# Layer 1 attention over chosen and near blocks: the loop takes two blocks of weights a step instead of one

## The chip, the cores and the metric

The kernel runs on one core of one Trainium2 chip. The metric is the time of one execution in microseconds. Three executions of the kernel before took 1608.29, 1609.14 and 1612.16 us (median 1609.14).

## The reference, cut to what matters

The program is a two-layer decoder trunk over 1024 tokens of width 1024. Layer 0 is a forgetting attention, layer 1 a sparse attention. In layer 1 each of 16 heads (four heads share keys and values) adds three branches: compressed keys, eight chosen blocks of 64 keys per token, and a window of the last 512 keys.

```python
o_s = softmax(q . k over the chosen blocks) @ v        # chosen
o_w = softmax(q . k over the last 512 keys) @ v        # near
o = g[..., 0:1] * o_c + g[..., 1:2] * o_s + g[..., 2:3] * o_w
x = x + (o.reshape(B, S, W) * silu(z)) @ w_out
```

The change is in the code that computes `o_s` and `o_w`. What is computed is the same before and after.

## The kernel before, in words

The work of layer 1 on `o_s` and `o_w` is cut into 32 "supers", one for each head and each half of 512 queries (`NsaSuper(h, s)`, for each head first s = 1, then s = 0). A super has two parts.

- Eight **units** (L1143), one for each branch and each tile of 128 queries. A unit multiplies queries with keys into a score tile `S_n` (two or four matmuls, L1162, into one of two score buffers of two PSUM banks), VectorE adds the mask and finds the minimum (L1169), ScalarE takes the exponential (L1170), VectorE the reciprocal of the sum (L1172), GpSimd scales by it and the gate (L1174). The weights `P_n` lie with queries on partitions.
- 12 **blocks** for s = 1 and 5 for s = 0, so 17 a head and 272 in all. A block is up to four 128 x 128 pieces of weights. `transposes` (L1180) turns them on TensorE into `ptp_n`, one of two PSUM banks (L1186). `split_t` (L140) then copies the bank to `pth_n` on ScalarE (L143) and writes the rest to `ptl_n` on VectorE (L144); each has four buffers. Only when VectorE has read the bank can the next block but one be transposed into it. `pv` (L1189) multiplies values with both parts into the super's output bank `O_n` (L1194, L1195). `finish` (L1197) reads `O_n` on ScalarE and VectorE (L1204, L1205) and frees it. Output banks are one of two, and the projection of z (`nz`) takes its accumulator from the same two.

`run_attn` (L162) writes these steps in order, with lag = 2 and late = 1: in step x the units of the next super that are due, the transposes of block x, the output products of block x - 2, and the finish of a super whose last block is x - 3. Meanwhile `merge` (L196) weaves in z's projection (`nz_n`, L131 to L133) at a fifth of the cost that the loop yields. The tile framework's scheduler then sets the order on each engine from this program and its own estimates, so instructions may stand in another order than they were written in; each engine runs its own list in order.

Of the kernel before, what the change touches and what calls it, by code (L numbers as in the profile page):

```python
# [38 lines left out]
def tile_fox_nsa(ctx, tc, a, out):  # L39
# [20 lines left out]
    def ps_a(name):  # L60
        return psA.tile([P, 512], F32, tag="A", name=name)
# [100 lines left out]
    def run_attn(supers, lead, lag, late):  # L162


        for u in supers[0].units():
            yield from u
        blocks = [(n, b) for n, x in enumerate(supers) for b in range(len(x.blocks))]
        todo, pend, po, units = 0, {}, {}, []
        for x in range(len(blocks) + lag + late):
            if x < len(blocks):  # L170
                n, b = blocks[x]
                sup = supers[n]
                if b == 0:
                    while todo < len(units):
                        yield from units[todo]
                        todo += 1
                    units, todo = (supers[n + 1].units() if n + 1 < len(supers) else []), 0
                while todo < len(units) and todo * len(sup.blocks) * lead <= b * len(units):
                    yield from units[todo]
                    todo += 1  # L180
                pend[x] = sup.transposes(b)
                yield 450
            if 0 <= x - lag < len(blocks):
                n, b = blocks[x - lag]
                if b == 0:
                    po[n] = ps_a(f"O_{supers[n].name}")
                supers[n].pv(po[n], b, *pend.pop(x - lag))
                yield 450
            if 0 <= x - lag - late < len(blocks):
                n, b = blocks[x - lag - late]  # L190
                if b == len(supers[n].blocks) - 1:
                    yield from supers[n].finish(po.pop(n))

# [67 lines left out]
    pend = []  # L261
# [850 lines left out]
    for qi in range(4):  # L1112
        n = P * (qi + 5)
        bias.append(at.tile([P, n], BF16, name=f"bias{qi}"))
        V.tensor_copy(bias[qi][:, n - P:n], tri)
    class NsaSuper:
# [80 lines left out]
        def finish(self, po):  # L1197
# [15 lines left out]
            yield 0  # L1213

    merge(run_attn([NsaSuper(h, s) for h in range(H) for s in (1, 0)], 0.9, 2, 1), filler, 0.2)
    at.release()
    kv[0].release()
# [110 lines left out]
```

## Time and profile before

| | us |
|---|---|
| median of three executions | 1609.14 |
| the profiled execution | 1609.73 |
| its span (first to last instruction) | 1607.7 |
| stretch of the loop, 1043 to 1505 us | 462 |
| TensorE busy in that stretch | 455.38 |
| VectorE busy in it | 396.13 |
| ScalarE busy in it | 360.80 |
| GpSimd busy in it | 255.88 |

The execution's own time is 2.0 us over the span. All that `run_attn` issues lies in the stretch from 1043 to 1505 us. A busy TensorE is counted from modelled ends of matmuls that overlap, so how fast it goes is read from the distance between the starts of two matmuls in the timeline, and what it waits for from the idle time before a weight load (PEld) or a matmul (PE).

### The profile page before, as it was taken

How to read it: one execution, taken by the hardware profiler on the slowest of the kernel's cores; microseconds unless marked ns; L12 is line 12 of the kernel's file. 1: busy time of each engine (PE TensorE's matmuls, PEld its weight loads, DVE VectorE, ACT ScalarE, POOL GpSimd, SP SyncE). 2: the span in 40 equal slices, each digit the busy share in tenths (PEclk: the TensorE clock that was granted, in tenths of full speed). 3: DMA queues.
4: the chain of work that ended last, by engine and by line, in shares of the span. 5: the costliest groups of instructions: out<-in, count | busy, mean ns of one | idle time of the engine just before them, and what ended most of it. 6: DMA issues, size and time to landing. Idle time of an engine off the chain costs nothing.

```text
span 1607.7 us, 26181 instructions
## 1 busy us (share of the span) xinstructions
PE 1527.3 (95%) x8600; PEld 1269.1 (79%) x8600; DVE 1132.1 (70%) x2867; ACT 870.4 (54%) x2126; POOL 545.1 (34%) x584
## 2 busy tenths in 40 slices
PE   6999999999999868999999989999999999999898
PEld 5887777777777656878888777788888888888786
DVE  6377777777777884355654686788888888888633
ACT  5255545555555662223232545578778778787522
POOL 3232223323223110032333223446646547554200
PEclk9999999999999979999999999999999999999999
DMA  7676666657657675441535645511312312212442
GB/s 241 226 143 134 128 160 131 153 113 149 156 114 160 151 153 165 133 155 60 162 104 154 218 151 193 204 54 63 122 53 66 119 40 79 73 40 93 147 148 92
DMA packets 237431, 209.11 MB, mean 130 GB/s; under 512 B 162737, under 2 KB 184497, under 8 KB 237041
## 3 DMA queue, kind: packets, MB, share of 16 engines
q1 hardware_dynamic: 237296, 207.46, 47.3%
q8 instruction: 68, 1.11, 0.3%
q14 instruction: 67, 0.54, 0.1%
HBM read 123.26 MB, written 46.20 MB: 105 GB/s over the span
## 4 chain that ended last, share of the span: by engine, by line
PE 60%; DVE 18%; ACT 9%; issue 7%; DMA 4%; POOL 1%; SPq 0%; DVEq 0%; POOLq 0%; ACTq 0%
PE ptp_n L1186 6%; PE S_n L1162 6%; DVE P L532 4%; PE y L131 3%; PE y L132 3%; PE y L133 3%; PE O_n L1195 3%; PE O_n L1194 3%; DVE hl L543 3%; ACT P L541 3%; DMA wo<-wD 1%; ACT cP L969 1%; PE nz L131 1%; ACT hl L542 1%; PE nz L132 1%
## 5 line engine op out<-in xcount | busy, mean ns | idle before, releaser
L1174 POOL TENSOR_SCALAR P_n<-P_n,l_n,gates 128x640 f32<-128x640 f32 (+7 forms) x256 | 200.9, 791 | 179.8 <-DVE l_n L1172 146.0
L541 ACT ACTIVATE P<-P,m 128x256 f32<-128x256 f32 (+1 forms) x192 | 117.0, 610 | 164.2 <-DVE m L532 163.8
L144 DVE TENSOR_TENSOR ptl_n<-ptp_n,pth_n 128x512 fp32r<-128x512 f32 (+1 forms) x272 | 181.4, 672 | 33.8 <-ACT pth_n L143 30.1
L1170 ACT ACTIVATE P_n<-P_n,m_n 128x640 f32<-128x640 f32 (+7 forms) x256 | 188.5, 737 | 24.9 <-DVE m_n L1169 22.8
L143 ACT CAST pth_n<-ptp_n 128x512 fp32r<-128x512 f32 (+1 forms) x272 | 153.8, 569 | 72.7 <-PE ptp_n L1186 71.5
L1186 PE MATMUL ptp_n<-ident,P_n 128*128 128x128 f32 x1056 | 167.1, 275 | 5.4 <-DVE ptl_n L144 3.6
L1162 PE MATMUL S_n<-nk,nq 128*128 128x320 f32 (+5 forms) x768 | 171.1, 333 | 0.2 <-DVE m_n L1169 0.2
L512 POOL TENSOR_TENSOR Bd<-B,tri 128x128 f32<-128x128 f32 x128 | 65.0, 509 | 302.3 <-DVE m L532 284.9
L1186 PEld LDWEIGHTS ptp_n<-ident,P_n 128*128 128x128 f32 x1056 | 124.4, 140 | 31.9 <-DVE ptl_n L144 9.3
L1194 PE MATMUL O_n<-pth_n,nv 128*128 128x512 f32 (+3 forms) x384 | 140.1, 369 | 1.0 <-DVE ot_n L1205 0.7
L543 DVE SCALAR_TENSOR_TENSOR hl<-P,hl 128x256 f16<-128x256 f32 (+1 forms) x192 | 126.4, 686 | 19.4 <-ACT hl L542 17.8
L1162 PEld LDWEIGHTS S_n<-nk,nq 128*128 128x128 f32 x768 | 128.0, 188 | 15.2 <-DVE m_n L1169 1.6
L1195 PE MATMUL O_n<-ptl_n,nv 128*128 128x512 f32 (+3 forms) x384 | 120.6, 338 | 0.1
L1169 DVE CUSTOM_DVE_ANT_0 P_n<-S_n,wmask 128x128 f32<-128x128 f32 (+1 forms) x192 | 113.3, 591 | 9.0 <-PE S_n L1162 4.1
L555 PE MATMUL O<-v,pT 128*128 128x192 bf16 x576 | 104.1, 255 | 12.3 <-DMA pT<-hl 10.8
L131 PE MATMUL y<-wo,oh 128*128 128x512 f32 x256 | 103.1, 403 | 9.0 <-ACT oh L627 4.0
L132 PE MATMUL y<-wo,oh 128*128 128x512 f32 x256 | 102.3, 400 | 0.0
L133 PE MATMUL y<-wo,ol 128*128 128x512 f32 x256 | 101.4, 397 | 0.0
L555 PEld LDWEIGHTS <-pT 128*128 128x128 f16 x576 | 57.4, 100 | 54.6 <-issue 40.4
L556 PE MATMUL O<-v,pT 128*128 128x128 bf16 x576 | 97.7, 224 | 0.0
L542 ACT ACTIVATE hl<-P 128x256 f16<-128x256 f32 (+1 forms) x192 | 92.5, 513 | 2.5 <-DMA pT<-hl 0.8
L1194 PEld LDWEIGHTS O_n<-pth_n,nv 128*128 128x128 f32 x384 | 72.6, 189 | 7.0 <-DVE ot_n L1205 1.3
(346 smaller groups left out, 4077.7 us busy)
## 6 DMA issues: line engine op xcount, KB each, us to landing
nq<-qD SPq DMA_DIRECT2D x64, 256.0 KB
B<-cD SPq DMA_DIRECT2D x16, 512.0 KB
wo<-wD SPq DMA_DIRECT2D x16, 512.0 KB
nq<-qD SPq DMA_DIRECT2D x64, 128.0 KB
of<-oF SPq DMA_DIRECT2D x14, 512.0 KB
x<-in_x_dram SPq DMA_DIRECT2D x8, 512.0 KB
wst_k<-in_fox_w_dram SPq DMA_DIRECT2D x8, 512.0 KB
wst_v<-in_fox_w_dram SPq DMA_DIRECT2D x8, 512.0 KB
```

The lines of the kernel that those rows point to most:

```text
L131: T.matmul(ps, wh, mh, start=first, stop=False, **kw)
L132: T.matmul(ps, wh, ml, start=False, stop=False, **kw)
L144: V.tensor_tensor(lo[:, 0:n], pt[:, 0:n], f(hi[:, 0:n]), OP.subtract)
L541: A.activation(L[:, 0:n], L[:, 0:n], AF.Exp, bias=init, scale=-1.0, accum_out=self.lr[:, col + c:col + c + 1])
L543: V.scalar_tensor_tensor(lo[:, cs], L[:, 0:n], UP, hi[:, cs], OP.mult, OP.subtract)
L555: T.matmul(po[:, 0:192], self.hT[:, b0 + k, :], v[:, self.j, k, :], start=(k == 0), stop=False)
L1162: T.matmul(ps[:, b, 0:w], self.q[x][:, qi * P:(qi + 1) * P], k[:, k0 + b * w:k0 + b * w + w], start=(x == 0), stop=(x == 1))
L1170: A.activation(L, L, AF.Exp, bias=m, scale=-1.0, accum_out=lr[:, 0, qi:qi + 1])
L1174: G.tensor_scalar(L, L, lr[:, 1, qi:qi + 1], gates[:, i, x:x + 1], OP.mult, OP.mult)
L1186: T.transpose(pt[:, (x + i) * P:(x + i + 1) * P], L[:, kb * P - k0:(kb + 1) * P - k0], ident)
L1194: T.matmul(po[:, d], v, hi[:, c], start=(b == i == 0), stop=False)
L1195: T.matmul(po[:, d], v, lo[:, c], start=False, stop=(b == len(self.blocks) - 1 and i == len(pieces) - 1))
```

## The change

A step of the loop now takes two blocks: first the units due for both, then the transposes of both (up to eight in a row), then the output products of two blocks, x - 2 and x - 1, then the finishes of blocks x - 3 and x - 2. The yields to `merge` are doubled accordingly. Nothing else is changed; lines behind L187 move down by 2.

```diff
-        for x in range(len(blocks) + lag + late):
-            if x < len(blocks):
-                n, b = blocks[x]
+        for x in range(0, len(blocks) + lag + late, 2):
+            for y in range(x, min(x + 2, len(blocks))):
+                n, b = blocks[y]
...
-                pend[x] = sup.transposes(b)
-                yield 450
-            if 0 <= x - lag < len(blocks):
-                n, b = blocks[x - lag]
+            for y in range(x, min(x + 2, len(blocks))):
+                n, b = blocks[y]
+                pend[y] = supers[n].transposes(b)
+            yield 900
+            for y in range(max(0, x - lag), min(x + 2 - lag, len(blocks))):
+                n, b = blocks[y]
...
-                supers[n].pv(po[n], b, *pend.pop(x - lag))
-                yield 450
-            if 0 <= x - lag - late < len(blocks):
-                n, b = blocks[x - lag - late]
+                supers[n].pv(po[n], b, *pend.pop(y))
+            yield 900
+            for y in range(max(0, x - lag - late), min(x + 2 - lag - late, len(blocks))):
+                n, b = blocks[y]
```

In the two programs' lists of instructions the first difference on any engine lies in this loop, and behind it the lists are the same again from the first part of the output projection on. In the names below, `n4_1` is head 4, half s = 1, and a further number is the block or, for `P` and `S`, the branch and the query tile.

The first place is TensorE in the middle of head 1, s = 1. Before, from the transposes of block 5:

```order
L1186 MATMUL ptp_n1_1_5_11106<-ident_72,P_n1_1_1_0_10913 128x128
L1186 MATMUL ptp_n1_1_5_11106<-ident_72,P_n1_1_1_1_10927 128x128
L1186 MATMUL ptp_n1_1_5_11106<-ident_72,P_n1_1_1_2_10949 128x128
L1186 MATMUL ptp_n1_1_5_11106<-ident_72,P_n1_1_1_3_10960 128x128
L131 MATMUL nz1_1_10989<-hT1_1_0_6788,whi_nz1_10397 128x512
L132 MATMUL nz1_1_10989<-hT1_1_1_6789,whi_nz1_10397 128x512
L133 MATMUL nz1_1_10989<-hT1_1_0_6788,wlo_nz1_10398 128x512
L1194 MATMUL O_n1_1_11060<-pth_n1_1_3_11080,nv_0_0_10388 128x512
L1195 MATMUL O_n1_1_11060<-ptl_n1_1_3_11081,nv_0_0_10388 128x512
L1162 MATMUL S_n1_0_1_0_11120<-nk_0_1_10390,nq0_1_0_10997 128x128
L1162 MATMUL S_n1_0_1_0_11120<-nk_0_1_10390,nq1_1_0_10998 128x128
L1186 MATMUL ptp_n1_1_6_11129<-ident_72,P_n1_1_1_0_10913 128x128
```

And in the changed kernel, from the transposes of the same block:

```order
L1188 MATMUL ptp_n1_1_5_11118<-ident_72,P_n1_1_1_0_10898 128x128
L1188 MATMUL ptp_n1_1_5_11118<-ident_72,P_n1_1_1_1_10912 128x128
L1188 MATMUL ptp_n1_1_5_11118<-ident_72,P_n1_1_1_2_10949 128x128
L1188 MATMUL ptp_n1_1_5_11118<-ident_72,P_n1_1_1_3_10974 128x128
L1188 MATMUL ptp_n1_1_6_11127<-ident_72,P_n1_1_1_0_10898 128x128
L1188 MATMUL ptp_n1_1_6_11127<-ident_72,P_n1_1_1_1_10912 128x128
L1188 MATMUL ptp_n1_1_6_11127<-ident_72,P_n1_1_1_2_10949 128x128
L1188 MATMUL ptp_n1_1_6_11127<-ident_72,P_n1_1_1_3_10974 128x128
L1196 MATMUL O_n1_1_11060<-pth_n1_1_3_11080,nv_0_0_10388 128x512
L1197 MATMUL O_n1_1_11060<-ptl_n1_1_3_11081,nv_0_0_10388 128x512
L1196 MATMUL O_n1_1_11060<-pth_n1_1_4_11089,nv_0_0_10388 128x512
L1197 MATMUL O_n1_1_11060<-ptl_n1_1_4_11090,nv_0_0_10388 128x512
```

The transposes of blocks 5 and 6 now stand together, and the output products of blocks 3 and 4 behind them.

The second place is VectorE at the border between the two halves of head 4, right behind the split of block 1 of s = 0. Before:

```order
L1205 SCALAR_TENSOR_TENSOR ot_n4_1_12575<-O_n4_1_12304,ot_n4_1_12575 64x512
L1169 ISA P_n5_1_0_2_12542,m_n5_1_0_2_12543<-S_n5_1_0_2_12541,bias2_10483 128x896
L1169 ISA m_n5_1_0_2_12543 128x1
L1172 RECIPROCAL l_n5_1_0_12490<-l_n5_1_0_12490 128x1
L1169 ISA P_n5_1_0_3_12553,m_n5_1_0_3_12554<-S_n5_1_0_3_12552,bias3_10485 128x1024
L1169 ISA m_n5_1_0_3_12554 128x1
L1172 RECIPROCAL l_n5_1_0_12490<-l_n5_1_0_12490 128x1
L1169 ISA P_n5_1_1_0_12579,m_n5_1_1_0_12580<-S_n5_1_1_0_12578,wmask_10475 128x640
L1169 ISA m_n5_1_1_0_12580 128x1
L144 TENSOR_TENSOR ptl_n4_0_2_12569<-ptp_n4_0_2_12563,pth_n4_0_2_12568 128x512
```

And in the changed kernel, at the same place:

```order
L1171 ISA P_n5_1_0_2_12542,m_n5_1_0_2_12543<-S_n5_1_0_2_12541,bias2_10483 128x896
L1171 ISA m_n5_1_0_2_12543 128x1
L1171 ISA P_n5_1_0_3_12553,m_n5_1_0_3_12554<-S_n5_1_0_3_12552,bias3_10485 128x1024
L1171 ISA m_n5_1_0_3_12554 128x1
L1171 ISA P_n5_1_1_0_12564,m_n5_1_1_0_12565<-S_n5_1_1_0_12563,wmask_10475 128x640
L1171 ISA m_n5_1_1_0_12565 128x1
L1174 RECIPROCAL l_n5_1_0_12490<-l_n5_1_0_12490 128x1
L1171 ISA P_n5_1_1_1_12575,m_n5_1_1_1_12576<-S_n5_1_1_1_12574,wmask_10475 128x640
L1171 ISA m_n5_1_1_1_12576 128x1
L1174 RECIPROCAL l_n5_1_0_12490<-l_n5_1_0_12490 128x1
L144 TENSOR_TENSOR ptl_n4_0_2_12594<-ptp_n4_0_2_12588,pth_n4_0_2_12593 128x512
L1207 SCALAR_TENSOR_TENSOR ot_n4_1_12611<-O_n4_1_12325,ot_n4_1_12611 64x512
```

The finish of the earlier half (`ot_n4_1`) has moved from right behind the split of block 1 to behind the split of block 2, past four score tiles and two reciprocals.

The third place is TensorE at the loop's end, from the last block's transposes on. Before:

```order
L1186 MATMUL ptp_n15_0_4_17120<-ident_72,P_n15_0_0_2_16912 128x128
L1186 MATMUL ptp_n15_0_4_17120<-ident_72,P_n15_0_0_3_16943 128x128
L1186 MATMUL ptp_n15_0_4_17120<-ident_72,P_n15_0_1_2_17014 128x128
L1186 MATMUL ptp_n15_0_4_17120<-ident_72,P_n15_0_1_3_17036 128x128
L1194 MATMUL O_n15_0_17101<-pth_n15_0_2_17097,nv_3_0_15145 128x384
L1195 MATMUL O_n15_0_17101<-ptl_n15_0_2_17098,nv_3_0_15145 128x384
L1194 MATMUL O_n15_0_17101<-pth_n15_0_2_17097,nv_3_0_15145 128x128
L1195 MATMUL O_n15_0_17101<-ptl_n15_0_2_17098,nv_3_0_15145 128x128
L1194 MATMUL O_n15_0_17101<-pth_n15_0_3_17114,nv_3_1_15149 128x384
L1195 MATMUL O_n15_0_17101<-ptl_n15_0_3_17115,nv_3_1_15149 128x384
L1194 MATMUL O_n15_0_17101<-pth_n15_0_3_17114,nv_3_1_15149 128x128
L1195 MATMUL O_n15_0_17101<-ptl_n15_0_3_17115,nv_3_1_15149 128x128
```

And in the changed kernel, at the same place:

```order
L1188 MATMUL ptp_n15_0_4_17118<-ident_72,P_n15_0_0_2_16912 128x128
L1188 MATMUL ptp_n15_0_4_17118<-ident_72,P_n15_0_0_3_16943 128x128
L1188 MATMUL ptp_n15_0_4_17118<-ident_72,P_n15_0_1_2_17014 128x128
L1188 MATMUL ptp_n15_0_4_17118<-ident_72,P_n15_0_1_3_17023 128x128
L1196 MATMUL O_n15_0_17101<-pth_n15_0_1_17086,nv_3_1_15136 128x512
L1197 MATMUL O_n15_0_17101<-ptl_n15_0_1_17087,nv_3_1_15136 128x512
L1196 MATMUL O_n15_0_17101<-pth_n15_0_2_17095,nv_3_0_15132 128x384
L1197 MATMUL O_n15_0_17101<-ptl_n15_0_2_17096,nv_3_0_15132 128x384
L1196 MATMUL O_n15_0_17101<-pth_n15_0_2_17095,nv_3_0_15132 128x128
L1197 MATMUL O_n15_0_17101<-ptl_n15_0_2_17096,nv_3_0_15132 128x128
L1196 MATMUL O_n15_0_17101<-pth_n15_0_3_17114,nv_3_1_15136 128x384
L1197 MATMUL O_n15_0_17101<-ptl_n15_0_3_17115,nv_3_1_15136 128x384
```

The output products of block 1 have moved behind the last transposes.

## Rows read from the trace of the kernel before

**Rows 1.** The page's busy time, share of the span and instructions of each engine.

```profile
PE 1527.3 (95%) x8600; PEld 1269.1 (79%) x8600; DVE 1132.1 (70%) x2867; ACT 870.4 (54%) x2126; POOL 545.1 (34%) x584
```

**Rows 2.** Windows: stretch and length, busy of PE, PEld, DVE, ACT, POOL, clock, DMA.

```profile
1043.00:1505.00 462.00, 455.38 (x2877) 400.40 (x2877) 396.13 (x1074) 360.80 (x820) 255.88 (x298) 1.00 0.22 72
...
1522.00:1530.00 8.00, 8.00 (x24) 6.24 (x24) 2.89 (x6) 3.46 (x7) 0.00 (x0) 0.64 0.59 163
```

**Rows 3.** Timeline, TensorE: start, length, engine, line, operation, tiles, shape, count.

```profile
1210.87 0.60 PE L1186 MATMUL ptp_n<-ident,P_n 128*128 128x128 f32 x4
1211.22 0.42 PE L1194 MATMUL O_n<-pth_n,nv 128*128 128x384 f32 x1
1211.48 0.33 PE L1195 MATMUL O_n<-ptl_n,nv 128*128 128x384 f32 x1
1211.65 0.22 PE L1194 MATMUL O_n<-pth_n,nv 128*128 128x128 f32 x1
1211.71 0.27 PE L1195 MATMUL O_n<-ptl_n,nv 128*128 128x128 f32 x1
1211.82 0.39 PE L1162 MATMUL S_n<-nk,nq 128*128 128x128 f32 x2
...
1212.33 0.39 PE L132 MATMUL nz<-hT,whi_nz 128*128 128x512 f32 x1
1212.56 0.40 PE L133 MATMUL nz<-hT,wlo_nz 128*128 128x512 f32 x1
```

**Rows 4.** Timeline, TensorE, near the loop's end.

```profile
1494.91 0.28 PE L1195 MATMUL O_n<-ptl_n,nv 128*128 128x128 f32 x1
1495.02 0.41 PE L1186 MATMUL ptp_n<-ident,P_n 128*128 128x128 f32 x2
```

**Rows 5.** Waits of weight loads in the loop's stretch: us in total, times, longest.

```profile
PEld ptp_n L1186 <- DVE ptl_n L144: 9.3, 28, 1.0
...
PEld S_n L1162 <- DVE m_n L1169: 1.6, 7, 0.5
PEld O_n L1194 <- DVE ot_n L1205: 1.3, 3, 0.8
```

**Rows 6.** Timeline, 1154.7 to 1157.3 us: a split that comes late.

```profile
1154.71 0.64 PE L1186 MATMUL ptp_n<-ident,P_n 128*128 128x128 f32 x4
...
1155.28 1.05 ACT L143 CAST pth_n<-ptp_n 128x512 fp32r<-128x512 f32 x2
...
1155.87 1.29 DVE L144 TENSOR_TENSOR ptl_n<-ptp_n,pth_n 128x512 fp32r<-128x512 f32 x2 [0.31 <-ACT pth_n L143]
...
1156.62 0.66 PE L1186 MATMUL ptp_n<-ident,P_n 128*128 128x128 f32 x4 [0.57 <-DVE ptl_n L144]
```

**Rows 7.** Timeline, the loop's last output products.

```profile
1502.22 0.69 DVE L144 TENSOR_TENSOR ptl_n<-ptp_n,pth_n 128x512 fp32r<-128x512 f32 x1 [1.00 <-ACT pth_n L143]
...
1502.50 0.33 PE L1194 MATMUL O_n<-pth_n,nv 128*128 128x256 f32 x1
...
1502.97 0.39 PE L1195 MATMUL O_n<-ptl_n,nv 128*128 128x256 f32 x1
```

**Rows 8.** Groups by line in the loop's stretch: busy us, mean ns, idle before.

```profile
L144 DVE TENSOR_TENSOR ptl_n<-ptp_n,pth_n 128x512 fp32r<-128x512 f32 (+1 forms) x272 | 181.4, 672 | 33.8 <-ACT pth_n L143 30.1
...
L1186 PE MATMUL ptp_n<-ident,P_n 128*128 128x128 f32 x1048 | 165.4, 275 | 5.2 <-DVE ptl_n L144 3.6 <-DVE l_n L1172 0.7 <-POOL P_n L1174 0.5
...
L1169 DVE CUSTOM_DVE_ANT_0 P_n<-S_n,bias 128x640 f32<-128x640 f32 (+3 forms) x60 | 61.0, 1017 | 4.1 <-PE ptp_n L1186 3.3 <-POOL P_n L1174 0.4
...
L1172 DVE RECIPROCAL l_n<-l_n 128x1 f32<-128x1 f32 x249 | 39.2, 158 | 15.0 <-ACT P_n L1170 11.8
L1205 DVE SCALAR_TENSOR_TENSOR ot_n<-O_n,ot_n 64x512 f32<-64x512 f32 x32 | 21.7, 678 | 1.8 <-ACT ot_n L1204 1.3
```

**Rows 9.** Timeline, VectorE: a score tile of 640 columns.

```profile
1210.59 0.82 DVE L1169 CUSTOM_DVE_ANT_0 P_n<-S_n,wmask 128x640 f32<-128x640 f32 x1 [0.37 <-POOL P_n L1174]
```

**Rows 10.** Timeline, TensorE: its first matmul behind 3.5 us of idle time.

```profile
1521.57 0.76 PE L131 MATMUL y<-wo,oh 128*128 128x512 f32 x1 [3.54 <-DVE xr L638]
```

## The prediction

> **What bounds the kernel now.** I read the page's busy shares first: TensorE leads with 95% of the span [rows 1]. Then the windows, since a mean over the span says little of one loop: in the loop's 462 us TensorE is busy for 455.38 us, VectorE for 396.13 (86%), ScalarE for 360.80, GpSimd for 255.88, at a granted clock of 1.00 [rows 2]. The reader is to see that TensorE never rests for long there and that VectorE is the next one, with 66 us of room. Then the timeline of TensorE, start to start. A matmul of 512 columns takes 0.23 us, one of 384 0.17, one of 128 0.06 when its partner follows [rows 3]; that is about 0.45 ns a column. Four transposes with the first output product of 384 columns take 0.61 us (1210.87 to 1211.48), which is 4 x 0.11 + 0.17: leaving a run of transposes costs nothing. Entering one costs 0.05 us where the matmul ahead has 128 columns (0.11 instead of 0.06 [rows 4]; the same before a score matmul [rows 3]), and nothing where it has more, since the next weight load then hides behind it.
>
> Last the waits. What weight loads wait for in the loop is small: 9.3 us in 28 places for the split on VectorE that empties the transposes' bank, 1.6 us for a score bank, 1.3 us for an output bank [rows 5]. How a late split looks: the casts of two blocks run back to back in 1.05 us behind exponentials, their VectorE halves take 1.29 us, and TensorE stands for 0.57 us before the transposes that need the first of the two banks [rows 6]. So the loop is bound by TensorE's own work, and the change does not touch the amount of that: the same 272 blocks, 256 units and matmuls. It can win or lose on borders between kinds of work and on waits.
>
> **The change part by part.**
> Borders. Counted in the two lists of TensorE's instructions, the loop enters a run of transposes 297 times before and 211 times now. Right behind a matmul of 128 columns it did so 56 times and does so 18 times: 38 x 0.05 = 1.9 us less. Matmuls of 128 columns ahead of a score or a z matmul go from 50 to 42: 8 x 0.05 = 0.4 us less. Together **-2.3 us**. The other borders cost nothing by the rows above, and bound the term: nothing is saved if weight loads turn out to be late all the same, and 4.3 us if each of the 86 entries that go is worth 0.05.
>
> The scheduler does the change by about half: 74 runs of six to eight transposes come out, 110 of four stay. That is in the counts above.
>
> Waits for the split. With the spacings above I added up TensorE's work between the end of a block's transposes and the start of those of the next block but one, which need its bank. Under 1.8 us there are 35 places before and 35 now; under 1.6 us there are 7 and 12. Five more tight places at the mean wait of 9.3 / 28 = 0.33 us are **+1.7 us**. In pairs the second block is not the tight one: under 1.8 us it stands once. Bounds: the 9.3 us go altogether, or each of the 74 pairs waits once for 0.57 us as at 1156.62, 42 us. I take the value near the first end, since the distances hardly move.
>
> Waits for score banks. Two units in a row stand 55 times in the new list, 18 times in the old; VectorE needs 0.67 us for a split and about 1.1 us for a large score tile [rows 8], so units in a row lean on the two score buffers. The distance from a unit to the next but one is under 1.0 us in 6 places instead of 5: 1.6 us x 6/5, **+0.3 us**. Bounds: -1.6 us, and 37 more double units at 1.6 / 7 = 0.23 us, +8.5 us.
>
> Waits of output products for the split. Between a block's transposes and its products TensorE now has 3.6 us of work in the middle of the distribution instead of 2.9. That hides what little is waited for; at the very end the last block's second product starts 0.47 us behind the first where 0.12 are due, because its split ends at 1502.91 [rows 7]. Two more products stand between now: **-0.3 us**.
>
> Other queues. No DMA is added; those that units and finishes issue on SP's queue move with them by a block at most, and in the loop the DMA engines are busy for 22% [rows 2]. Loads that the output projection waits for are set off by z's last matmul, which is the last TensorE work of the loop in both lists, so the end moves with TensorE. GpSimd has the scaling of weights in the same order; its room is 206 us.
>
> Sum: -2.3 + 1.7 + 0.3 - 0.3 = -0.6 us. Against the profiled execution's 1609.73 us that is 1609.1; it ran 0.6 us above the median of the three, so I predict **1608.5 us**.
>
> **The rivals.**
> *The waits go.* If a longer path between transposes and products lets the splits run ahead, the 9.3 us for the bank, the 1.3 us for output banks and most of the 1.6 us go: 12 us less, and no 2.0 us of new ones. 1608.5 - 14 is 1595 at most; with half of it 1601. For it: products wait less by the counts. Against: the bank's distances are no longer than before, and the bank, not the products, is where most is waited for.
>
> *The finish comes late at the middle of a head (slower).* In heads 2, 4, ... 14 the border between the halves falls between two pairs. There the list of VectorE has the finish behind two splits, four score tiles, two reciprocals and a third split. The queue from block 0's split on is 3 x 0.67 + 2 x (1.02 + 0.08) + 2 x (0.82 + 0.08) + 3 x 0.16 + 0.68 = 7.2 us [rows 8, 9] (0.08 us is what reading the minimum adds), and at its head two more score tiles of 1.1 us each are still under way, some 1.3 us of them. So the output bank is free some 8.5 us after the transposes of block 0 start. TensorE has until then 19 transposes, six products, six units and ten z matmuls, 9.2 us by the spacings, and then wants the bank. The margin is 0.7 us. It decides from there: VectorE also waits in this stretch, for casts (33.8 us of idle time before splits in the loop) and exponentials (15.0 before reciprocals) [rows 8]. If it slips by 2 us, TensorE stands 1.3 us at seven heads and about as much for the score banks behind it, 9 us: 1617.5 us.
>
> *The change does nothing* because the scheduler pulls the pairs apart again: 1609 us. Against it, 74 long runs.
>
> *The clock falls.* Granted were 1.00 in the whole loop, where runs of four transposes (0.44 us) stand between matmuls; behind 3.54 us of idle TensorE at 1521.57 [rows 10] the clock went to the lower level (1.2 GHz), 0.64 on average over 8 us [rows 2], a loss of 2.9 us. Runs of eight would need 0.88 us without another matmul, far from that idle time; if the clock fell once a head, 16 x 2.9 = 46 us, 1655 us. The Trainium skill ("TensorE: Matmul & The Clock Gate", Part 4: PE-mode transpose) says that a transpose does not count as TensorE activity for the clock gate and takes about 275 ns in a kernel. The mean here is 275 ns [rows 8], as it says; that transposes let the clock fall no run here shows, and by that rule this rival would come true where runs double.
>
> **How the numbers follow.** A change below 0.3% (4.8 us) cannot be told from none. Forecast 0.66 and the change that does nothing 0.08, both within 0.3% (1604.3 to 1614.0), less 0.01 for the forecast's own edge below it: same 0.73. The waits go 0.12, with that edge faster 0.13. The late finish 0.12 and the clock 0.02: slower 0.14. The forecast's own range is 1604 to 1613. For 8 in 10 I reach a third into each of the two likelier rivals: 1601 to 1616, which leaves out about 0.18.
>
> **What would show it.** In the changed profile: the loop's stretch again 459 to 466 us at a clock of 1.00; transposes in runs of eight at 0.11 us start to start; the wait of weight loads for the split (L144) between 8 and 14 us, for score banks about 2; the last products 0.12 us apart. If the waits for the split fall below 5 us the first rival is right; if products wait for the finish (L1207) for over 5 us, or score matmuls for the minimum (L1171), the second. I am wrong if the stretch differs by over 5 us, or if the difference lies outside of it.

## The result and the profile after

The changed kernel takes 1617.51 us (median of six runs, 1615.64 to 1619.63), the kernel before 1608.72 in the same comparison: 1.0053 times as long, with a 95% interval of 1.0038 to 1.0068. It is 8.8 us slower, outside of the range that was forecast and on the other side. Its profiled execution took 1619.63 us.

First the page's busy line of the changed kernel, to be laid beside [rows 1]:

```profile
PE 1537.7 (95%) x8600; PEld 1270.4 (79%) x8600; DVE 1135.4 (70%) x2867; ACT 865.8 (54%) x2126; POOL 547.6 (34%) x584
```

Then the windows between two landmarks that both kernels have, from the first output product behind the first 384- and 512-column score tiles of head 0 to the first matmul of the output projection (columns as in [rows 2]). Before:

```profile
1043.04:1505.95 462.91, 456.30 (x2880) 401.16 (x2881) 396.09 (x1074) 360.76 (x820) 256.77 (x299) 1.00 0.22 72
```

After:

```profile
1044.86:1519.29 474.43, 464.38 (x2881) 401.94 (x2881) 399.24 (x1074) 356.52 (x821) 256.84 (x298) 1.00 0.22 70
```

The same instructions take 11.5 us longer, at the same clock. So the loss lies in the loop. (Each kernel left one profile, so these are two single executions.) Outside of it the two profiles differ by +1.8 us ahead and -3.1 us behind; in the profiles taken below the first transposes stand anywhere from 1033 to 1040 us in kernels that differ only behind them, and the stretch behind the loop takes 97 to 102 us, so one pair of profiles says nothing there.

What TensorE waits for in that stretch after (us in total, times, longest; before: [rows 5]):

```profile
PEld ptp_n L1188 <- DVE ptl_n L144: 11.2, 34, 0.7
PEld S_n L1164 <- DVE m_n L1171: 6.7, 23, 1.1
PE ptp_n L1188 <- DVE ptl_n L144: 6.4, 21, 0.5
PEld ptp_n L1188 <- POOL P_n L1176: 5.6, 13, 0.7
PEld O_n L1196 <- DVE ot_n L1207: 2.0, 8, 0.3
```

These rows are not yet the loss: a weight load's wait (PEld) counts even where a matmul still runs in front of it, and what the matmul behind it waits stands in a row of its own (PE). The row with POOL P_n names GpSimd, but wherever a block's first transpose comes over 0.05 us late in the loop, its weights were scaled before the bank's split ended; it is the bank there, too. I took the distance between the starts of neighbouring matmuls over the loop and subtracted the spacings of [rows 3, 4]. What is left over, before and after, in us, by the matmul that starts late:

| late matmul | before | after |
|---|---|---|
| first transpose of a block right behind another block's transposes | 0.2 (3 places) | 5.3 (20) |
| other transposes inside a run (0.05 each, mostly) | 1.5 | 2.5 |
| first transpose behind another kind of work | 10.7 | 11.2 |
| product behind a product | 1.6 | 5.3 |
| score matmul | 4.8 | 7.5 |
| all (with z and the rest) | 24.3 | 38.0 |

That is 13.7 us more, and the spacings themselves sum to some 2 us less. Of the transposes' 12.4 and 19.0 us, the split that empties the bank accounts for 11.5 and 18.4. Two places show the two rows that grew most. The first, on ScalarE, VectorE and TensorE, from 1441.83 us:

```profile
1441.83 0.58 ACT L143 CAST pth_n<-ptp_n 128x512 fp32r<-128x512 f32 x1
...
1442.30 0.73 ACT L1172 ACTIVATE P_n<-P_n,m_n 128x512 f32<-128x512 f32 x1
...
1443.01 0.58 ACT L143 CAST pth_n<-ptp_n 128x512 fp32r<-128x512 f32 x1
...
1443.61 0.38 PE L1188 MATMUL ptp_n<-ident,P_n 128*128 128x128 f32 x2
1443.62 0.69 DVE L144 TENSOR_TENSOR ptl_n<-ptp_n,pth_n 128x512 fp32r<-128x512 f32 x1 [0.28 <-ACT pth_n L143]
...
1444.46 0.63 PE L1188 MATMUL ptp_n<-ident,P_n 128*128 128x128 f32 x4 [0.47 <-DVE ptl_n L144]
```

The pair's first block has two transposes, which start at 1443.61, so the second block's four are due at 1443.83. But the bank that they need still holds the second block of the pair before. Its cast stands on ScalarE behind the first one's cast and behind an exponential; it starts at 1443.01, VectorE's half behind it ends at 1444.31, and TensorE goes on at 1444.46, 0.63 us late.

Other work in the queue is the rule. In 16 places a pair's second block starts over 0.1 us late, 5.1 us in sum. In 14 of them (4.7 us) something else stands ahead of the split that empties the bank, which ends 2.0 to 3.3 us behind its last transpose: on ScalarE exponentials in ten places and the read of an output bank in one, on VectorE score tiles in three. Only two places (0.4 us) show the bare chain of cast and VectorE half, 1.57 us.

The second place, TensorE's products of two blocks:

```profile
1323.45 0.22 PE L1196 MATMUL O_n<-pth_n,nv 128*128 128x128 f32 x1
1323.51 0.27 PE L1197 MATMUL O_n<-ptl_n,nv 128*128 128x128 f32 x1
1323.62 0.39 PE L1196 MATMUL O_n<-pth_n,nv 128*128 128x384 f32 x1
1323.85 0.34 PE L1197 MATMUL O_n<-ptl_n,nv 128*128 128x384 f32 x1
```

The 128-column product at 1323.51 is followed after 0.11 us instead of 0.06, and the next block's 384-column product takes 0.23 instead of 0.17. A product right behind another block's 128-column product stands 42 times in the loop now and stood 6 times before: 0.05 us each, and 0.055 more in the 26 where 384 columns follow, 0.05 more in the 16 where 256 do (0.17 instead of 0.12 us).

### The profile page after: what moved, and what is told of

Its sections match the earlier page's. It is cut to its first block, busy times and chain, and to the rows that moved or that the text cites. A ratio compares the mean times of both kernels' runs of the same rounds, so it can differ in the third digit from the quotient of the medians.

```text
span 1617.9 us, 26138 instructions
## 1 busy us (share of the span) xinstructions
PE 1537.7 (95%) x8600; PEld 1270.4 (79%) x8600; DVE 1135.4 (70%) x2867; ACT 865.8 (54%) x2126; POOL 547.6 (34%) x584
## 4 chain that ended last, share of the span: by engine, by line
PE 60%; DVE 19%; ACT 9%; issue 6%; DMA 4%; POOL 1%; SPq 0%; DVEq 0%; ACTq 0%; POOLq 0%
PE S_n L1164 7%; PE ptp_n L1188 6%; DVE P L534 4%; PE y L131 3%; PE y L132 3%; PE y L133 3%; PE O_n L1196 3%; PE O_n L1197 3%; DVE hl L545 3%; ACT P L543 3%; ACT cP L971 1%; ACT hl L544 1%; PE nz L131 1%; PE nz L132 1%; PE nz L133 1%
## 5 line engine op out<-in xcount | busy, mean ns | idle before, releaser
L144 DVE TENSOR_TENSOR ptl_n<-ptp_n,pth_n 128x512 fp32r<-128x512 f32 (+1 forms) x272 | 180.0, 671 | 37.8 <-ACT pth_n L143 35.8
L1164 PE MATMUL S_n<-nk,nq 128*128 128x320 f32 (+5 forms) x768 | 165.5, 334 | 1.2 <-DVE m_n L1171 1.0
L1188 PE MATMUL ptp_n<-ident,P_n 128*128 128x128 f32 x1056 | 156.0, 276 | 7.8 <-DVE ptl_n L144 6.4
L1188 PEld LDWEIGHTS ptp_n<-ident,P_n 128*128 128x128 f32 x1056 | 121.0, 141 | 35.1 <-DVE ptl_n L144 11.2
L1196 PE MATMUL O_n<-pth_n,nv 128*128 128x512 f32 (+3 forms) x384 | 131.7, 352 | 0.1
L557 PE MATMUL O<-v,pT 128*128 128x192 bf16 x576 | 104.0, 255 | 12.7 <-DMA pT<-hl 11.2
```

The costliest lines, as they stand in the source:

```text
L144: V.tensor_tensor(lo[:, 0:n], pt[:, 0:n], f(hi[:, 0:n]), OP.subtract)
L1164: T.matmul(ps[:, b, 0:w], self.q[x][:, qi * P:(qi + 1) * P], k[:, k0 + b * w:k0 + b * w + w], start=(x == 0), stop=(x == 1))
L1188: T.transpose(pt[:, (x + i) * P:(x + i + 1) * P], L[:, kb * P - k0:(kb + 1) * P - k0], ident)
L1196: T.matmul(po[:, d], v, hi[:, c], start=(b == i == 0), stop=False)
```

## The experiments

Theory 1: the second block of a pair waits for its bank, because splits queue up. Theory 2: borders between products cost time. The rivals stand in the expectations. Fifteen kernels ran; times are medians, and ratios are to the kernel before on the same chip (1607.7 to 1609.1 us).

**Which part of the step costs time.** Four kernels. *Units alone in twos*:

```diff
-            for y in range(x, min(x + 2, len(blocks))):
-                n, b = blocks[y]
-                pend[y] = supers[n].transposes(b)
-            yield 900
...
+            for d in range(2):
+                y = x + d
+                if y < len(blocks):
+                    n, b = blocks[y]
+                    pend[y] = supers[n].transposes(b)
+                    yield 450
+                y -= lag
+                if 0 <= y < len(blocks):
...
+                    supers[n].pv(po[n], b, *pend.pop(y))
+                    yield 450
```

> Only the units come in twos: a step issues the units of two blocks, then block x's transposes, the output products of block x - 2, block x + 1's transposes and the products of x - 1. In TensorE's list 17 pairs of blocks have their transposes side by side (before 5, changed kernel 81), 5 products stand right behind another block's 128-column product (6 and 42), and two units in a row stand 51 times (18 and 55). Theory 1 (the second block of a pair waits for its bank, because VectorE needs 0.67 us a split and TensorE only 0.44 us for four transposes: 7.7 us of such waits in the changed kernel, 1.4 before) and theory 2 (products of two blocks side by side expose a weight load, 0.05 us in 42 places and 0.055 more in 28, some 3.3 us): within 3 us of the kernel before, 1607 to 1612. Rival 3 (score banks, because units come in twos): as slow as the changed kernel, 1615 to 1619.

Measured: 1609.79 us, 1.0005 (0.9994 to 1.0017). No loss that can be told, so units in twos alone do not make the changed kernel slow, as rival 3 had it. They are not free, though. In this kernel's profile the loop, from its first transpose to the projection, is 3.5 us longer than before; weight loads wait 8.2 us for score banks instead of 1.6 [rows 5], and first transposes behind another kind of work start 8.2 us late in sum instead of 10.7:

```profile
PEld S_n L1167 <- DVE m_n L1174: 8.2, 23, 1.1
```

*Output products alone in twos*:

```diff
             for y in range(x, min(x + 2, len(blocks))):
...
                     todo += 1
-            for y in range(x, min(x + 2, len(blocks))):
-                n, b = blocks[y]
                 pend[y] = supers[n].transposes(b)
-            yield 900
+                yield 450
```

> Only the output products come in twos: units and transposes of each block stand together as before, two blocks a step, and then come the products of two blocks. 28 pairs of transposes side by side, 40 products behind another block's 128-column product, two units in a row 20 times. By the spacings of the kernel before TensorE's work without waits is 2.8 us shorter. Theory 1: the waits of second blocks fall from 7.7 to about 3 us; with theory 2's 3.3 us the time is that of the kernel before within 2.5 us, 1607 to 1611. If theory 2 held alone, as slow as the changed kernel (1615 to 1619); if theory 1 held alone, 1604 to 1608. Rival 3: no loss.

Measured: 1614.68 us, 1.0037 (1.0026 to 1.0047). More than forecast, and neither theory's number. Products behind products lose 4.6 us, nearly what they lose in the changed kernel, and second blocks only 1.1. But first blocks lose 15.3 us instead of 10.7, which no theory had said.

*Transposes in twos, products apart*, with the second block's products behind the next step's units; units come in twos here too:

```diff
...
+            for y in range(max(0, x - lag - 1), min(x - lag, len(blocks))):
+                n, b = blocks[y]
...
+                supers[n].pv(po[n], b, *pend.pop(y))
+                yield 450
             for y in range(x, min(x + 2, len(blocks))):
                 n, b = blocks[y]
                 pend[y] = supers[n].transposes(b)
             yield 900
-            for y in range(max(0, x - lag), min(x + 2 - lag, len(blocks))):
+            for y in range(max(0, x - lag), min(x + 1 - lag, len(blocks))):
...
```

> Only the transposes come in twos: the products of the second block of a step are issued behind the next step's units, so products are apart. 87 pairs of transposes side by side, 14 products behind another block's 128-column product, two units in a row 49 times; the distance from a block's transposes to those of the next block but one is under 1.6 us in 28 places (changed kernel 12). Theory 1: slow, 1614 to 1620, with waits of second blocks of 7 us or more. Theory 2 alone: 1607 to 1611.

Measured: 1623.36 us, 1.0093 (1.0076 to 1.0111), slower than the changed kernel. Second blocks lose 5.6 us, as theory 1 says; the score banks lose much too, so this is not the price of transposes in twos alone. Its row of waits for them, beside 1.6 us before [rows 5]:

```profile
PEld S_n L1170 <- DVE m_n L1177: 13.5, 39, 1.1
```

*Pairs that start anew at each head*:

```diff
-        for x in range(0, len(blocks) + lag + late, 2):
-            for y in range(x, min(x + 2, len(blocks))):
+        starts = [v for v in range(len(blocks)) if v % 17 % 2 == 0]
+        groups = [list(range(v, w)) for v, w in zip(starts, starts[1:] + [len(blocks)])]
...
+        for i in range(len(groups) + 2):
+            for y in groups[i] if i < len(groups) else ():
...
```

> The changed kernel, but the pairs start anew at each head: 17 blocks are eight pairs and a single one, so that no pair of an odd head straddles the border between two halves or two heads. 80 pairs of transposes side by side, 34 products behind another block's 128-column product, two units in a row 62 times. Theories 1 and 2: as slow as the changed kernel, 1615 to 1620 (distances under 1.6 us: 27 instead of 12). Rival 4 (the loss comes where pairs straddle, in the odd heads: in the trace a pair of heads loses 1.6 us, all of it between the starts of an odd head and the next): 1608 to 1611.

Measured: 1616.65 us, 1.0050 (1.0034 to 1.0067). The loss stays, so it does not hang on pairs that straddle a border.

**More pairs.** *Products ahead of the transposes in a step*:

```diff
-            for y in range(x, min(x + 2, len(blocks))):
-                n, b = blocks[y]
-                pend[y] = supers[n].transposes(b)
-            yield 900
             for y in range(max(0, x - lag), min(x + 2 - lag, len(blocks))):
...
                 supers[n].pv(po[n], b, *pend.pop(y))
             yield 900
+            for y in range(x, min(x + 2, len(blocks))):
+                n, b = blocks[y]
+                pend[y] = supers[n].transposes(b)
+            yield 900
```

> The changed kernel with a step's products ahead of its transposes. The list has more pairs: 109 blocks' transposes stand right behind another's (changed kernel 81), 40 products behind another block's 128-column product. Theory 1: waits of second blocks grow with their number, from 7.7 to about 10 us: 1617 to 1623. If pairing as such were not the cause but the place of the products, no slower than the changed kernel: under 1616.

Measured: 1633.89 us, 1.0160 (1.0144 to 1.0176). Slower than any theory had it, and by another wait: second blocks lose 1.0 us, but products now come before their weights are split. What changed is the distance, not the split: from a block's last transpose to its first product there are 1.99 us in the median instead of the changed kernel's 4.03, and the split ends 1.97 us behind that transpose instead of 2.00.

```profile
PEld O_n L1196 <- ACT pth_n L143: 20.3, 57, 0.8
PEld O_n L1197 <- DVE ptl_n L144: 9.1, 33, 0.5
```

So this kernel says nothing for or against theory 1; it shows that products need the distance that the changed kernel's order gives them.

**Is it the split?** Each of the next four alterations was made to both kernels, and the gap between the two is what tells. *VectorE's half reads the rounded copy instead of the bank*:

```diff
-            return split_t(at, pt, n * P, f"{self.name}_{b}")
...
+            A.copy(hi[:, 0:n * P], pt[:, 0:n * P])
+            V.tensor_tensor(lo[:, 0:n * P], f(hi[:, 0:n * P]), f(hi[:, 0:n * P]), OP.subtract)
...
```

> The kernel before, in which VectorE's half of the split reads the rounded copy twice instead of the transposes' bank, so that the second part of the weights is zero and the bank is free behind ScalarE's cast. All instructions stay in number. The cast ends some 0.85 us behind the last transpose instead of 1.74 for the split, so the 11.5 us that transposes wait for banks go nearly all: 1597 to 1601.

> The same alteration of the changed kernel. Theory 1 and 2: the 18.4 us of bank waits go, the 3.3 us of exposed loads between products stay, so the kernel is 2 to 4 us slower than the altered kernel before: 1599 to 1605. Rival 5 (it is not the banks: what pairing costs lies in the longer stretches without transposes or units, on GpSimd and the score banks): the gap to the altered kernel before stays 8 us or more.

Measured: 1639.18 (1.0192, 1.0176 to 1.0208) and 1646.83 us (1.0236, 1.0220 to 1.0252). Both were slower by far, so the pair is no clean test. The gap between the two stayed at 7.7 us by the medians, just under the 8 of rival 5, though no bank waited for VectorE's half. The groups by line of the altered kernel before (busy us, mean ns) show what got slower:

```profile
L1174 POOL TENSOR_SCALAR P_n<-P_n,l_n,gates 128x512 f32<-128x512 f32 (+2 forms) x235 | 242.7, 1039 | 136.7 <-DVE l_n L1172 101.0 <-PE ptp_n L1186 13.8 <-PE S_n L1162 9.1
L1190 DVE TENSOR_TENSOR ptl_n<-pth_n 128x512 fp32r<-128x512 f32 (+1 forms) x252 | 210.3, 840 | 24.2 <-ACT pth_n L1189 21.8
```

The same group on GpSimd in the kernel before, where VectorE reads one of its two inputs from the bank (its own half: [rows 8], 672 ns):

```profile
L1174 POOL TENSOR_SCALAR P_n<-P_n,l_n,gates 128x384 f32<-128x384 f32 (+2 forms) x250 | 195.1, 787 | 175.1 <-DVE l_n L1172 141.3 <-PE ptp_n L1186 18.4 <-PE S_n L1162 15.0
```

With both inputs in SBUF, VectorE's half takes 840 ns and GpSimd's scaling 1039 instead of 787.

*No reciprocals on VectorE*:

```diff
-            V.reciprocal(lr[:, 1, qi:qi + 1], lr[:, 0, qi:qi + 1])
             x = 3 * h + 1 + y
-            G.tensor_scalar(L, L, lr[:, 1, qi:qi + 1], gates[:, i, x:x + 1], OP.mult, OP.mult)
+            G.tensor_scalar(L, L, lr[:, 0, qi:qi + 1], gates[:, i, x:x + 1], OP.mult, OP.mult)
```

> The kernel before without VectorE's 256 reciprocals (GpSimd scales by the sum itself, so the weights are scaled wrongly): 40 us less work in VectorE's queue, and no waiting for an exponential there. TensorE's work is the same. Bank waits fall from 11.5 us to 6 to 9, score-bank waits to under 2: 1603 to 1608.

> The same alteration of the changed kernel, with 80 pairs of transposes side by side and 39 products behind another block's 128-column product. Theory 1a (the second block waits for the chain itself: two casts of 0.57 us and two VectorE halves of 0.67 us back to back behind transposes that follow each other in 0.44 us, however free VectorE is): waits of second blocks stay at 6 us or more, the gap to the altered kernel before at 6 to 10 us: 1610 to 1617. Theory 1b (VectorE's queue of other work makes the second split late): these waits fall below 4 us and the gap to the 2 to 5 us of the borders: 1606 to 1612.

Measured: 1609.03 (0.9999, 0.9986 to 1.0011) and 1618.42 us (1.0056, 1.0038 to 1.0075). A gap of 9.4 us, so these 40 us of VectorE's other work are not the cause of it. Theory 1b holds in half at most: second blocks did fall below 4 us, to 3.5, but the gap did not fall. The kernel before did not get faster, against my forecast for it.

*VectorE's half over half of the columns*, with second parts in four tiles zeroed ahead of the loop:

```diff
-            return split_t(at, pt, n * P, f"{self.name}_{b}")
...
+            A.copy(hi[:, 0:n * P], pt[:, 0:n * P])
+            V.tensor_tensor(lo[:, 0:n * 64], pt[:, 0:n * 64], f(hi[:, 0:n * 64]), OP.subtract)
...
```

> The kernel before, in which VectorE's half of the split covers only the first half of a block's columns (the other columns of the second part stay zero): some 0.37 us instead of 0.67, 272 times, still read from the transposes' bank. TensorE's and ScalarE's work stay. A lone block's bank is free 0.3 us sooner: bank waits fall from 11.5 us to 2 to 5, 1600 to 1606.

> The same alteration of the changed kernel. The list has 114 pairs of transposes side by side (changed kernel 81). Theory 1a (a second block waits for the chain of two casts and two VectorE halves): the second half now ends 0.37 us behind the second cast, some 1.35 us behind the block's last transpose instead of 1.8, so waits of second blocks fall from 7.7 to under 3 us, in spite of more pairs, and the gap to the altered kernel before to the borders' 2 to 5 us: 1602 to 1610. If the second blocks' waits have another cause: a gap of 8 us or more.

Measured: 1607.95 (0.9995, 0.9983 to 1.0006) and 1617.50 us (1.0053, 1.0038 to 1.0067). The half took 0.41 us, not 0.37, as the group by line of the altered changed kernel shows:

```profile
L1197 DVE TENSOR_TENSOR ptl_n<-ptp_n,pth_n 128x256 fp32r<-128x256 f32 (+1 forms) x265 | 108.6, 413 | 53.3 <-ACT pth_n L1196 50.3
```

In the profiles the loop, from its first transpose to the projection, is 3.6 and 5.8 us shorter than without the alteration, but the zeroing on VectorE stands ahead of it, and the whole times did not move. The gap stayed at 9.5 us. Here theory 1a failed: the gap should have fallen to 2 to 5 us, and second blocks, 114 of them instead of 81, still lose 3.8 us.

*No VectorE half at all*:

```diff
-            return split_t(at, pt, n * P, f"{self.name}_{b}")
...
+            A.copy(hi[:, 0:n * P], pt[:, 0:n * P])
+            return hi, zlo
```

> The kernel before without VectorE's half of the split: the second part of the weights is one tile of zeros, and the products with it still run. TensorE's and ScalarE's work stay, VectorE has 181 us less, and a bank is free behind ScalarE's cast, some 0.85 us behind the last transpose. Nothing is read twice from SBUF, so GpSimd is not slowed as in the kernel that read the rounded copy twice. The waits for banks go (11.5 us) and most of the score banks': 1595 to 1600.

> The same alteration of the changed kernel; 125 pairs of transposes side by side. By the spacings its list is 3.9 us shorter than that of the altered kernel before, and the borders between products cost some 3.5 us. If what pairing costs beyond the borders lies in the queue of splits, on ScalarE and VectorE: within 3 us of the altered kernel before, 1595 to 1602. If it lies elsewhere: a gap of 7 us or more.

Measured: 1605.76 (0.9980, 0.9969 to 0.9991) and 1607.83 us (1.0001, 0.9990 to 1.0011). The gap falls from 0.53% to 0.21%, or from 8.8 to 2.1 us by the medians, although this list has 125 pairs instead of 81 and the same borders. What waits for the split is now ScalarE's cast alone, in the changed kernel:

```profile
PEld ptp_n L1191 <- ACT pth_n L1193: 5.1, 8, 0.8
PE ptp_n L1191 <- ACT pth_n L1193: 4.2, 9, 0.6
```

But it is not the second blocks' waits that went. They are 4.2 us here (5.3 in the changed kernel), nearly all in seven places, and in each of the seven exponentials stand on ScalarE ahead of the cast that is waited for. The loop's gap went from 11.6 to 4.1 us in the profiles, and over half of that at products behind another kind of work, because the kernel before loses more there without VectorE's half: they start 7.3 us late in sum instead of 2.7, much of it for output banks, and in the changed kernel 2.5 instead of 1.8. The altered kernel before:

```profile
PEld O_n L1199 <- DVE ot_n L1210: 5.8, 13, 0.6
```

So the smaller gap does not show that the loss goes through VectorE's half. That the kernel before got only some 3 us faster, where 9 to 14 were forecast, fits with this: its 11.5 us of bank waits were in good part replaced by others.

**Attempts at a faster kernel**, both one block a step. *Units a little later*, lead 1.0 instead of 0.9:

```diff
-    merge(run_attn([NsaSuper(h, s) for h in range(H) for s in (1, 0)], 0.9, 2, 1), filler, 0.2)
+    merge(run_attn([NsaSuper(h, s) for h in range(H) for s in (1, 0)], 1.0, 2, 1), filler, 0.2)
```

> An attempt at a faster kernel: one block a step as before, with units due a little later (lead 1.0 instead of 0.9). The distance from a block's transposes to those of the next block but one is under 1.8 us in 25 places instead of 35; 34 products stand behind another block's wide product, where nothing is exposed. Theory 1: some 3 us less of bank waits, 1604 to 1608. If the distances don't decide: 1607 to 1611.

Measured: 1612.70 us, 1.0029 (1.0017 to 1.0041), slower: the transposes' bank waits were 12.5 us instead of 11.5 in spite of the longer distances.

*More of z's work behind the transposes that wait*:

```diff
                 pend[x] = sup.transposes(b)
-                yield 450
+                yield 1800 if len(sup.blocks) == 12 and b in (1, 2, 7) else 181
```

> An attempt at a faster kernel, one block a step as before: the loop yields more behind the transposes of blocks 1, 2 and 7 of each s = 1 half and less behind the others, so that z's matmuls stand where transposes wait for banks. The distance from a block's transposes to those of the next block but one is under 1.8 us in 21 places instead of 35, under 1.6 in 4 instead of 7, all else in the list as before. Theory 1: bank waits fall from 11.5 us to some 8, 1604 to 1608. If the waits only move: 1608 to 1611.

Measured: 1607.27 us, 0.9993 (0.9979 to 1.0007), no difference that can be told. The bank waits fell to 7.8 us, and the products' waits for the output bank rose (weight loads for L1205: 1.3 [rows 5] to 3.7 us). Neither of the two beat the kernel before.

## Why the prediction was wrong, point by point

- *TensorE's own work bounds the loop* held: the clock stayed at 1.00, the work stayed the same, and the difference lies in the loop. The rivals that the clock falls and that the change does nothing fall, and so does the one that the waits go: they grew. (The Trainium skill, "TensorE: Matmul & The Clock Gate", Part 4, says that transposes do not count as activity for the clock gate; with runs of eight the granted clock was 1.00 all the same, so nothing here bears it out.) The last products start 0.12 us apart, as forecast [rows 7]:

```profile
1517.48 0.28 PE L1196 MATMUL O_n<-pth_n,nv 128*128 128x256 f32 x1
1517.60 0.28 PE L1197 MATMUL O_n<-ptl_n,nv 128*128 128x256 f32 x1
```

- *Waits for the split, +1.7 us*: this step failed. I compared distances between transposes with one latency, 1.6 to 1.8 us, for every block, and said that "in pairs the second block is not the tight one". Second blocks lose 5.3 us instead of 0.2. In the trace after, a second block's VectorE half ends some 2.4 us behind its last transpose in the median, that of the others 1.8; and in the 14 places above, where other work stood ahead of it, the split that is waited for took 2.0 to 3.3 us. In 13 of the 16 late places TensorE's own work fills over 1.8 us between the two, where I had counted no wait. The count was off as well: by the same spacings a second block stands under 1.8 us in 11 places, not once. I had such a late split before me, behind exponentials, in [rows 6], and the bound of 42 us from it, and set it aside.
- *Borders, -2.3 us*: the 38 borders to transposes are gone (the spacings sum to some 2 us less), but 36 to another block's product came in their place, at 0.05 us and 0.05 more on the matmul behind; products behind products lose 3.7 us more in all. Of the 0.4 us for score and z matmuls most was never there: I left out that 7 borders now lead from a 128-column score matmul to another score tile.
- *Score banks, +0.3 us*: mis-sized; score matmuls start 2.7 us later in sum, and weight loads wait 6.7 us for these banks instead of 1.6. Units in twos alone bring that wait (8.2 us), though the whole time did not show it.
- *My sign for the waits was a bad one*: I wrote 8 to 14 us of weight loads waiting for L144, and found 11.2, in the middle of it. What grew is what TensorE itself waits for (3.6 to 6.4 us); before:

```profile
PE ptp_n L1186 <- DVE ptl_n L144: 3.6, 10, 0.7
```

- *The late finish* names 1617.5 us, what was measured, but the match is chance: its output-bank wait is 2.0 us in 8 places of up to 0.3, not 1.3 at seven heads, and with pairs aligned to heads the loss stays. Its other sign, over 5 us of score matmuls waiting for the minimum (6.7), came true without its mechanism.

Shown by the two traces is where the 11.5 us lie: second blocks 5.1, products behind products 3.7, score matmuls 2.7, other transposes 1.5, the rest 0.7, less 2.2 of spacings. Shown by the runs is that products in twos are enough for a loss (1.0037), and that transposes in twos with units in twos beside them are (1.0093). Not shown is what makes the second block's split late. Without reciprocals, with half of VectorE's half and with none of it, second blocks still lost 3.5, 3.8 and 4.2 us. The work that stood ahead of the split most often, ScalarE's exponentials, was taken away in no run, so that cause is read from the traces only. Open too is what each of the terms would be worth alone, since every kernel that undid one moved waits to another buffer.

## What to carry to other kernels

Work that is put in twos leaves a fixed number of buffers in twos: ask for the second of a pair when its chain ends, with the first one's steps and the engines' other work in line ahead of it, not what a lone one takes. Count a border against what comes to stand there, not only against what goes. And read lost time from start-to-start distances; a weight load's wait may hide behind a running matmul, and a wait taken away often comes back at the next buffer.

## What the runs showed of the hardware

VectorE's half of the split took 840 ns in the mean with both inputs in SBUF, where it took 672 with one input in PSUM, and GpSimd's scaling beside it rose from 787 to 1039 ns. The kernel before was 31 us slower with no other change in its text. The Trainium skill ("GPSIMD Engine Reference", section 1, Specifications) says that GpSimd shares SBUF interfaces with VectorE and contends with its instructions of two SBUF inputs; the runs agree, in that both got slower together.
